# A hybrid decoder layer on one core: the first norm's factor from a token-layout copy of x, and another order of the first two projections

## The chip, the cores and the metric

One core of one Trainium2 chip runs the kernel. The metric is the device time of one execution in microseconds (us); lower is better. An instruction here runs on TensorE (PE: matrix products; PEld is its weight load), VectorE (DVE), ScalarE (ACT) or GpSimd (POOL); SyncE (SP) issues the DMA transfers. Each engine takes its instructions in the order in which the program gives them, and waits where an operand isn't there.

## The reference

`x` is 256 tokens of 1024 channels, in float32; the depth is one layer. The parts of the reference that matter here:

```python
def rms_norm(x, g):
    y = x * rsqrt(mean(x * x, axis=-1) + 1e-6)
    return y * g
...
h = rms_norm(x, pre_mix_g)                 # the first norm
u = h @ w_in                               # 1024 -> 2560 columns, split among four mixers
y_a = conformer_conv_mixer(u[:, :512])     # val * sigmoid(gate), causal conv of 31 taps, group norm, silu
...
y = concat([y_a, y_b, y_c, y_d]) @ w_out
x = x + rms_norm(y, post_mix_g)
m = square(relu(rms_norm(x, pre_mlp_g) @ mlp_w1)) @ mlp_w2
x = x + rms_norm(m, post_mlp_g)
```

The factor of the first norm, `rsqrt(mean(x*x) + eps)`, is one number for each token. It commutes with the projection, so the kernel multiplies it in after the product.

## The kernel before, in words

**Layout.** The first half of the kernel works in channel layout: 128 channels on the partitions, 256 tokens along a row. The weights come in chunks of 128 x 2048 float32 (1 MB) in the order of `seq` (line 87): ten chunks of `w_in`, four of `w_out`, then `w1` and `w2` in turn. Chunk number n is loaded by `load(n)` (SP), copied to a rounded half by `split_hi(n)` (ACT), and the rest is taken by `split_lo(n)` (DVE, `raw - hi`). A projection `proj(n)` (line 320) then makes three products for each of 8 channel blocks k and each of its two halves j: hi x hT, hi x hL, lo x hT, 48 products of 128x256 in all; `hT` and `hL` are the rounded half and the rest of `x * pre_mix_g`. So the third product of a half needs that half of the chunk's `lo`.

**Chunk 0** is different: its weights `w0` to `w7` come in the head (`hd`, lines 137 to 140, seven transfers) beside the blocks `x0` to `x7` of x in channel layout, and `native(k)` (line 189) makes its products in full float32, as four PE instructions for each k.

**The first norm's factor.** ACT squares the x blocks in pairs (`square`, line 208), DVE adds the results (`add`, line 211), and two products with a column of ones (`pss`, lines 254 to 256) sum over the partitions, which gives the sum of squares of each token on a partition. ACT takes the root with a scale and a bias, DVE the reciprocal (`rstd`), PE spreads it along a row with two transposes (`pr`, lines 261 to 263), and ACT copies that row to `R1` and its square to `R2`. In PE's order the `pss` products stand behind `native(4)`, the transposes behind `native(5)`.

**The first gate.** `conf_gate(t)` (line 364) multiplies a projection's gate half by `R1` on DVE into a tile `g` and takes its sigmoid on ACT. `conf_val(t)` (line 370) multiplies the value half by `R1` into the same tile `g`, which so has to wait for the sigmoid, then by the sigmoid into `zpad`, and ACT begins the convolution (`cacc`). The convolution's other taps (`run_taps`) fill DVE's time later.

**Order.** `InOrder` (line 50) keeps every engine's instructions in program order; the program is written out by hand at lines 555 to 659. Projections write to PSUM tiles of the tag `mm`, of which there are two, used in turn: `pu[3]`, the result of `proj(3)`, takes the place of `pu[1]` and so cannot be started before `conf_val(1)`, which stands behind `split_lo(3)` on DVE, has read `pu[1]`.

**Later.** `x` in token layout (`xs`, 2 x 512 KB) is loaded at lines 637 and 638 for the first residual. At the end (lines 957 to 964) PE makes twenty products of four shapes into a PSUM tile that nothing reads.

Of the kernel before, what the change touches and what calls it, by code (L numbers as in the profile page):

```python
# [16 lines left out]
F32 = mybir.dt.float32  # L17
F32R = mybir.dt.float32r
BF16 = mybir.dt.bfloat16
AF = mybir.ActivationFunctionType  # L20
ALU = mybir.AluOpType
# [3 lines left out]
P = 128  # L25
S = 256
D = 1024
KT = D // P
# [37 lines left out]
def hybrid_layer(ctx, tc, x, head, win, wout, w1, w2, gates, rows, out):  # L66
    nc = tc.nc
    V, A, G, T, Q = (InOrder(tc, e) for e in (nc.vector, nc.scalar, nc.gpsimd, nc.tensor, nc.sync))
# [4 lines left out]
    few = ctx.enter_context(tc.tile_pool(name="few", bufs=2))  # L73
    wk_ctx = tc.tile_pool(name="wk", bufs=1)
    wk = wk_ctx.__enter__()
# [4 lines left out]
    def sm(name):  # L80
        return psm.tile([P, 512], F32, tag="sm", name=name)

    def mm(name):
        return pmm.tile([P, 512], F32, tag="mm", name=name)


    seq = [("in", c) for c in (0, 1, 8, 5, 6, 7, 9, 3, 4, 2)]
# [6 lines left out]
    raw, hi, lo = {}, {}, {}  # L94

    def new_raw(n):
        k = seq[n]
        raw[k] = wts.tile([P, NW], F32, tag="raw", name=f"raw_{k[0]}{k[1]}")
        return raw[k], src[k[0]][k[1]]

    def load(n, parts=1):
        if n < len(seq):
            w, d = new_raw(n)
            for i in range(parts):
                c = slice(i * NW // parts, (i + 1) * NW // parts)
                Q.dma_start(w[:, c], d[:, c])

    def part(i, parts):
        return slice(i * NW // parts, (i + 1) * NW // parts)

    def split_hi(n, i=0, parts=1):
        if n < len(seq):
            k = seq[n]
            if i == 0:
                hi[k] = wts.tile([P, NW], F32R, tag="hi", name=f"hi_{k[0]}{k[1]}")
            c = part(i, parts)
            A.activation(hi[k][:, c], raw[k][:, c], AF.Copy)

    def split_lo(n, i=0, parts=1):
        if n < len(seq):  # L120
            k = seq[n]
            if i == 0:
                lo[k] = wts.tile([P, NW], F32R, tag="lo", name=f"lo_{k[0]}{k[1]}", bufs=3)
            c = part(i, parts)
            V.tensor_tensor(lo[k][:, c], raw[k][:, c], hi[k][:, c].bitcast(F32), op=ALU.subtract)
# [8 lines left out]
    xs = [cst.tile([P, D], F32, name=f"x{t}") for t in range(2)]  # L134
    gw = wk.tile([P, 4, P], F32, name="gw")
    c = 0
    for blocks in HEAD:
        n = HOFF[blocks[-1]] + S
        Q.dma_start(hd[:, c:n], head[:, c:n])
        c = n  # L140

    def hb(b):
        return hd[:, HOFF[b]:HOFF[b] + S]

    def xpair(k):
        a, b = HOFF[f"x{k}"], HOFF[f"x{k + 1}"] - HOFF[f"x{k}"]
        return hd[:, a:a + 2 * b].rearrange("p (k c) -> p k c", c=b)[:, :, :S]

    load(1, 2)
    load(2, 2)  # L150
    load(3)

# [2 lines left out]
    warm = cst.tile([P, 256], BF16, name="warm")  # L155
# [8 lines left out]
    eps_r = cst.tile([P, 1], F32, name="eps_r")  # L164
# [3 lines left out]
    ones = cst.tile([P, 1], F32, name="ones")  # L168
    G.memset(ones, 1.0)
    ident = cst.tile([P, P], F32, name="ident")  # L170
# [7 lines left out]
    hF = wts.tile([P, KT, S], F32, tag="hi", name="hF")  # L178
    hT = big.tile([P, KT, S], F32R, tag="hT", name="hT")
    hL = big.tile([P, KT, S], F32R, tag="hL", name="hL")  # L180
    sq = [wk.tile([P, 2, 2, S], F32, name="sq", tag=t) for t in ("sqx", "pTs")]
    sq = [q[:, i] for q in sq for i in range(2)]

    def bank(b, name):
        return mm(name) if b < 0 else pacc.tile([P, 512], F32, tag=f"acc{b}", name=name)

    pu0 = [bank(b, f"pu0_{j}") for j, b in enumerate((-1, 0))]

    def native(k):
        for j in range(2):  # L190
            T.matmul(pu0[j][:, :S], hb(f"w{k}")[:, j * P:(j + 1) * P], hF[:, k, :], start=(k == 0), stop=(k == KT - 1))
# [7 lines left out]
    e = wk.tile([P, 2], F32, name="e")  # L199
    sr = wk.tile([P, 2], F32, name="sr")  # L200
    s2 = wk.tile([P, 2], F32, name="s2")
    q = wk.tile([P, 2], F32, name="q_")
    A.preload_act_table(AF.Exp)

    def hf(k):
        V.tensor_scalar(hF[:, k, :], hb(f"x{k}"), hd[:, C_PRE + k:C_PRE + k + 1], None, op0=ALU.mult)

    def square(k):
        A.activation(sq[k // 2], xpair(k), AF.Square)

    def add(a, b):
        V.tensor_tensor(a, a, b, op=ALU.add)

    def h_hi(k):
        A.activation(hT[:, k:k + 2, :], hF[:, k:k + 2, :], AF.Copy)

    def h_lo(k):
        V.tensor_tensor(hL[:, k:k + 2, :], hF[:, k:k + 2, :], hT[:, k:k + 2, :].bitcast(F32), op=ALU.subtract)
# [1 line left out]
    hf(0)  # L220
    hf(1)
    V.tensor_scalar(nl, lam, -1.0, None, op0=ALU.mult)
    square(0)
    h_hi(0)
    hf(2)
    V.tensor_tensor(ab, nl, lam, op=ALU.max)
    A.activation(e, ab, AF.Exp, scale=-1.0)
    G.tensor_copy(prm, hd[:, :PCOLS])
    hf(3)
    square(2)  # L230
    hf(4)
    add(sq[0], sq[1])
    square(4)
    h_hi(2)
    hf(5)
    add(sq[0], sq[2])
    square(6)
    A.preload_act_table(AF.Sqrt)
    hf(6)
    hf(7)  # L240
    add(sq[0], sq[3])
    V.tensor_scalar(sr, e, 2.0, None, op0=ALU.add)
    add(sq[0][:, 0], sq[0][:, 1])
    V.reciprocal(sr, sr)
    h_hi(4)
    h_hi(6)
    h_lo(0)
    h_lo(2)
    for k in range(5):
        native(k)  # L250
    R1 = cst.tile([P, S], F32, name="R1")
    R2 = cst.tile([P, S], F32, name="R2")
    rstd = cst.tile([P, 2], F32, name="rstd")
    pss = sm("pss")
    for t in range(2):
        T.matmul(pss[:, t:t + 1], sq[0][:, 0, t * P:(t + 1) * P], ones, start=True, stop=True)
    A.activation(rstd, pss[:, 0:2], AF.Sqrt, bias=eps_r, scale=1.0 / D)
    V.reciprocal(rstd, rstd)
    h_lo(4)
    native(5)  # L260
    pr = sm("pR")
    for t in range(2):
        T.transpose(pr[:, t * P:(t + 1) * P], rstd[:, t:t + 1].to_broadcast([P, P]), ident)
    native(6)
    native(7)

    zpad = wk.tile([P, 2, CK - 1 + S], F32, name="zpad")
    G.memset(zpad[:, :, :CK - 1], 0.0)
# [4 lines left out]
    identb = cst.tile([P, P], BF16, name="identb")  # L273
# [43 lines left out]
    def two(pu):  # L317
        return pu.rearrange("p (j t) -> p j t", j=2)

    def proj(n, between=None):  # L320
        c = seq[n][1]
        pu = mm(f"pu{c}")
        H, L = hi["in", c], lo["in", c]
        for j in range(2):
            if j and between:
                between()
            o = pu[:, j * S:(j + 1) * S]
            for k in range(KT):
                ws = slice(j * 1024 + k * P, j * 1024 + (k + 1) * P)
                T.matmul(o, H[:, ws], hT[:, k, :], start=(k == 0), stop=False)  # L330
                T.matmul(o, H[:, ws], hL[:, k, :], start=False, stop=False)
                T.matmul(o, L[:, ws], hT[:, k, :], start=False, stop=(k == KT - 1))
        return two(pu)

    def proj_v(n):
# [28 lines left out]
    def conf_gate(t):  # L364
        g = st["cg", t] = wk.tile([P, S], F32, name="cg", tag="la")
        V.tensor_tensor(g, pu[t][0], R1, op=ALU.mult)
        s = st["sig", t] = wk.tile([P, S], F32, name="sig", tag="lt")
        A.activation(s, g, AF.Sigmoid)

    def conf_val(t):  # L370
        g = st["cg", t]
        V.tensor_tensor(g, pu[t][1], R1, op=ALU.mult)
        V.tensor_tensor(zpad[:, t, CK - 1:], g, st["sig", t], op=ALU.mult)
# [42 lines left out]
    def scaled(o, pu, r=None):  # L416
        V.tensor_tensor(o, pu, (R1 if r is None else r)[:, None, :].to_broadcast([P, 2, S]), op=ALU.mult)

# [136 lines left out]
    pu = {}  # L555

    load(4)
    split_hi(1, 0, 2)
    A.activation(R1, pr[:, :S], AF.Copy)
    split_lo(1, 0, 2)  # L560
    h_lo(6)
    split_hi(1, 1, 2)
    A.preload_act_table(AF.Sigmoid)
    A.activation(R2, R1, AF.Square)
    pu[0] = [p_[:, :S] for p_ in pu0]
    conf_gate(0)
    split_lo(1, 1, 2)

    pu[1] = proj(1)
    pu[1] = [pu[1][:, t] for t in range(2)]  # L570
    split_hi(2, 0, 2)
    conf_val(0)
    split_hi(2, 1, 2)
    split_lo(2, 0, 2)
    run_taps(2, 0)
    split_lo(2, 1, 2)
    split_hi(3)

    pu[2] = proj(2)
# [54 lines left out]
    att_ptrans()  # L634
    run_taps(2)
    lru_scan()
    Q.dma_start(xs[0], x[0:P, :])
    Q.dma_start(xs[1], x[P:, :])

    pu[8] = proj(8)  # L640
    split_lo(9)
# [195 lines left out]
    wk = ctx.enter_context(tc.tile_pool(name="wk2", bufs=2))  # L837
# [41 lines left out]
    cols = {(t, h): half(h) for t in range(2) for h in range(2)}  # L879
# [7 lines left out]
    for n in range(14, len(seq)):  # L887
        name, c = seq[n]
# [10 lines left out]
        if n == 14:  # L899

            for t in range(2):
                scr = few.tile([P, D], BF16, name="scr", bufs=1)
# [52 lines left out]


    pb = mm("shapes")
    H15 = hi["w2", 15]
    wide_zeros = warm[:, None, :].to_broadcast([P, 2, 256])
    for lhs, rhs, n in ((H15[:, :P], H15[:, 512:1024], 512), (identb, wide_zeros, 512), (H15[:, :P], H15[:, 512:896], 384),  # L960
                        (H15[:, :P], H15[:, 512:576], 64)):
        for _ in range(5):
            T.matmul(pb[:, :n] if rhs is not wide_zeros else pb.rearrange("p (a b) -> p a b", a=2), lhs, rhs,
                     start=True, stop=True)


# [41 lines left out]
```

## Time and profile before

| what | value |
|---|---|
| median of 3 runs | 288.17 us (287.48 to 288.68) |
| profiled execution, its own time | 288.29 us |
| span of that execution, first to last instruction | 286.6 us |
| PE busy | 279.3 us, 97% |
| DVE busy | 193.6 us, 68% |
| ACT busy | 152.6 us, 53% |
| POOL busy | 22.3 us, 8% |
| DMA | 53.04 MB, mean 185 GB/s |

A timeline row gives the start, the duration, the engine, the line, the operation and its tiles (out <- in), the shapes, and after x how many instructions the row merges; brackets hold idle time of the engine just before and what ended it. All instructions carry line 60, since one helper issues them, so the tiles tell them apart. A matmul's end is modelled; its start is what counts. A DMA row gives the number of issues, KB of each and the median time from issue to landing.

### The profile page before, as it was taken

The numbers are of one execution on the slowest core, as the hardware profiler recorded it, in microseconds if no ns is written. First come the engines' busy times: TensorE is split into PE (matmuls) and PEld (weight loads), VectorE is DVE, ScalarE is ACT, GpSimd is POOL, SyncE is SP. The second block draws the span as 40 slices with busy tenths as digits, with TensorE's granted clock in tenths as the row PEclk, the third lists the DMA queues.
The fourth block names the chain that finished last, engine by engine and source line by source line (L and its number), as shares of the span: only waits on it lengthen the run. The fifth ranks groups of instructions, "written<-read, shape, count | busy, mean of one in ns | idle before, by whom it ended". The sixth has DMA issues, their size and how long they took to land.

```text
span 286.6 us, 4726 instructions
## 1 busy us (share of the span) xinstructions
PE 279.3 (97%) x1954; PEld 255.9 (89%) x1954; DVE 193.6 (68%) x262; ACT 152.6 (53%) x192; POOL 22.3 (8%) x53
## 2 busy tenths in 40 slices
PE   6799999999999999999999999999999999999995
PEld 4699997999977899989999899899899899899883
DVE  1999999899989996765636646546447357257262
ACT  3995459875548849642632623624615515526141
POOL 4388500000000000000000000000000000000000
PEclk9999999999999999999999999999999999999999
DMA  6999446926404544675374383472472562600012
GB/s 210 412 409 334 150 156 225 411 74 238 146 2 153 213 150 173 266 287 214 101 281 166 129 293 133 165 293 96 199 287 74 226 255 69 266 0 0 2 73 74
DMA packets 9237, 53.04 MB, mean 185 GB/s; under 512 B 1024, under 2 KB 1536, under 8 KB 3712
## 3 DMA queue, kind: packets, MB, share of 16 engines
q1 hardware_dynamic: 9216, 52.75, 49.1%
q8 instruction: 15, 0.25, 0.3%
q14 instruction: 6, 0.05, 0.1%
HBM read 51.70 MB, written 1.05 MB: 184 GB/s over the span
## 4 chain that ended last, share of the span: by engine, by line
PE 94%; DMA 2%; DVE 1%; SPq 0%; ACT 0%; issue 0%
PE acd L60 31%; PE pm L60 29%; PE pu L60 19%; PE acc L60 7%; DMA hd<-in_head_dram 2%; PE pz L60 2%; PE shapes L60 1%; PE psc L60 1%; PE po L60 1%; DVE sq L60 1%; PE pg L60 1%; PE pth L60 0%; PE ptp L60 0%; SPq L60 0%; PE pvar L60 0%; DVE hF L60 0%
## 5 line engine op out<-in xcount | busy, mean ns | idle before, releaser
L60 DVE TENSOR_TENSOR lo_w<-raw_w,hi_w 128x2048 fp32r<-128x2048 f32 (+2 forms) x36 | 72.6, 2050 | 17.8 <-ACT hi_w L60 17.8
L60 PE MATMUL pm<-h2L,hi_w 128*128 128x256 f32 x240 | 66.5, 277 | 0.0
L60 PE MATMUL pm<-h2T,hi_w 128*128 128x256 f32 x240 | 66.5, 277 | 0.0
L60 PE MATMUL pm<-h2T,lo_w 128*128 128x256 f32 x240 | 66.4, 277 | 0.0
L60 ACT ACTIVATE hi_w<-raw_w 128x2048 fp32r<-128x2048 f32 (+1 forms) x33 | 59.6, 1849 | 1.3 <-issue 1.3
L60 PE MATMUL acd<-hi_w,ml 128*128 128x512 f32 (+1 forms) x160 | 56.0, 350 | 0.0
L60 PE MATMUL acd<-lo_w,mh 128*128 128x512 f32 (+1 forms) x160 | 55.8, 349 | 0.0
L60 PE MATMUL acd<-hi_w,mh 128*128 128x512 f32 (+1 forms) x160 | 55.8, 348 | 0.0
L60 ACT ACTIVATE mr<-pm 128x512 f32<-128x512 f32 x15 | 8.9, 596 | 73.8 <-PE pm L60 73.8
L60 PEld LDWEIGHTS pm<-h2T,hi_w 128*128 128x128 f32 x240 | 45.1, 188 | 0.0
L60 PEld LDWEIGHTS pm<-h2T,lo_w 128*128 128x128 f32 x240 | 45.1, 188 | 0.0
L60 PEld LDWEIGHTS pm<-h2L,hi_w 128*128 128x128 f32 x240 | 45.1, 188 | 0.0
L60 DVE TENSOR_TENSOR mr<-mr 128x512 f32<-128x512 f32 x16 | 11.1, 693 | 44.7 <-ACT mr L60 44.7
L60 PE MATMUL pu<-hT,hi_in 128*128 128x256 f32 x128 | 36.3, 284 | 0.0
L60 PE MATMUL pu<-hT,lo_in 128*128 128x256 f32 x128 | 35.9, 280 | 0.0
L60 PE MATMUL pu<-hL,hi_in 128*128 128x256 f32 x128 | 35.9, 280 | 0.0
L60 PEld LDWEIGHTS acd<-lo_w,mh 128*128 128x128 f32 x160 | 30.2, 189 | 4.2
L60 PEld LDWEIGHTS acd<-hi_w,ml 128*128 128x128 f32 x160 | 30.1, 188 | 4.2
L60 PEld LDWEIGHTS acd<-hi_w,mh 128*128 128x128 f32 x160 | 30.1, 188 | 4.1
L60 DVE SCALAR_TENSOR_TENSOR cacc<-zpad,prm,cacc 128x256 f32<-128x256 f32 x60 | 25.3, 477 | 0.1
L60 PEld LDWEIGHTS pu<-hT,hi_in 128*128 128x128 f32 x128 | 24.3, 190 | 0.0
L60 PEld LDWEIGHTS pu<-hT,lo_in 128*128 128x128 f32 x128 | 24.2, 189 | 0.0
(177 smaller groups left out, 381.3 us busy)
## 6 DMA issues: line engine op xcount, KB each, us to landing
raw_w<-in_w_dram SPq DMA_DIRECT2D x32, 1024.0 KB, 4.9
raw_in<-in_win_dram SPq DMA_DIRECT2D x7, 1024.0 KB, 5.6
raw_out<-in_wout_dram SPq DMA_DIRECT2D x4, 1024.0 KB, 4.9
raw_in<-in_win_dram SPq DMA_DIRECT2D x4, 512.0 KB, 7.9
hd<-in_head_dram SPq DMA_DIRECT2D x3, 384.0 KB, 5.9
x<-in_x_dram SPq DMA_DIRECT2D x2, 512.0 KB, 7.5
grow<-in_rows_dram SPq DMA_DIRECT2D x2, 512.0 KB, 7.1
hd<-in_head_dram SPq DMA_DIRECT2D x2, 256.0 KB, 4.9
```

The costliest lines, as they stand in the source:

```text
L60: ins = f(*args, **kwargs)
```

## The change

It loads x in token layout early, between chunk 1 and chunk 2, and no longer at lines 637 and 638. The squares, adds and ones-products go; ACT squares each of the two token tiles with a running sum instead (`token_rstd`). The products of chunk 0 stand in one go on PE. Chunk 1's products (`proj_passes`) go pass by pass, all hi x hT of a half, then all hi x hL, then all lo x hT, with the transposes behind the first pass of the second half. The `hi` of chunk 1 is made as two quarters and a half, and chunk 2's first half is split ahead of `conf_gate(0)`, its second half behind it. Chunk 0's two PSUM tiles are `acc0` and `acc1` instead of one `mm` and `acc0`. The unread products at the end are six of 256 columns, one of 2, six of 256 and six of 512.

```diff
     load(1, 2)
+    for t in range(2):
+        Q.dma_start(xs[t], x[t * P:(t + 1) * P, :])
     load(2, 2)
     load(3)
...
-    sq = [wk.tile([P, 2, 2, S], F32, name="sq", tag=t) for t in ("sqx", "pTs")]
-    sq = [q[:, i] for q in sq for i in range(2)]
...
-    pu0 = [bank(b, f"pu0_{j}") for j, b in enumerate((-1, 0))]
+    pu0 = [bank(b, f"pu0_{j}") for j, b in enumerate((0, 1))]
...
     hf(3)
-    square(2)
-    hf(4)
-    add(sq[0], sq[1])
-    square(4)
+    A.preload_act_table(AF.Sqrt)
     h_hi(2)
-    hf(5)
-    add(sq[0], sq[2])
-    square(6)
-    A.preload_act_table(AF.Sqrt)
-    hf(6)
-    hf(7)
-    add(sq[0], sq[3])
-    V.tensor_scalar(sr, e, 2.0, None, op0=ALU.add)
-    add(sq[0][:, 0], sq[0][:, 1])
-    V.reciprocal(sr, sr)
+    for k in range(4, KT):
+        hf(k)
     h_hi(4)
     h_hi(6)
-    h_lo(0)
-    h_lo(2)
-    for k in range(5):
+    V.tensor_scalar(sr, e, 2.0, None, op0=ALU.add)
+    V.reciprocal(sr, sr)
+    for k in range(KT):
         native(k)
+    for k in range(0, KT, 2):
+        h_lo(k)
...
-    pss = sm("pss")
-    for t in range(2):
-        T.matmul(pss[:, t:t + 1], sq[0][:, 0, t * P:(t + 1) * P], ones, start=True, stop=True)
-    A.activation(rstd, pss[:, 0:2], AF.Sqrt, bias=eps_r, scale=1.0 / D)
-    V.reciprocal(rstd, rstd)
-    h_lo(4)
-    native(5)
-    pr = sm("pR")
-    for t in range(2):
-        T.transpose(pr[:, t * P:(t + 1) * P], rstd[:, t:t + 1].to_broadcast([P, P]), ident)
-    native(6)
-    native(7)
+    def token_rstd():
+        ss0 = few.tile([P, 2], F32, name="ss0", bufs=1)
+        for t in range(2):
+            scr = few.tile([P, D], BF16, name="scr", bufs=1)
+            A.activation(scr, xs[t], AF.Square, accum_out=ss0[:, t:t + 1])
+        A.activation(rstd, ss0, AF.Sqrt, bias=eps_r, scale=1.0 / D)
+        V.reciprocal(rstd, rstd)
+    def row_of_rstd():
+        pr = sm("pR")
+        for t in range(2):
+            T.transpose(pr[:, t * P:(t + 1) * P], rstd[:, t:t + 1].to_broadcast([P, P]), ident)
+        A.activation(R1, pr[:, :S], AF.Copy)
+        A.activation(R2, R1, AF.Square)
...
+    def proj_passes(n, between):
+        c = seq[n][1]
+        pu = mm(f"pu{c}")
+        H, L = hi["in", c], lo["in", c]
+        for j in range(2):
+            o = pu[:, j * S:(j + 1) * S]
+            for i, (w, h) in enumerate(((H, hT), (H, hL), (L, hT))):
+                for k in range(KT):
+                    ws = slice(j * 1024 + k * P, j * 1024 + (k + 1) * P)
+                    T.matmul(o, w[:, ws], h[:, k, :], start=(i == 0 and k == 0), stop=(i == 2 and k == KT - 1))
+                if j and i == 0:
+                    between()
+        return two(pu)
...
     load(4)
-    split_hi(1, 0, 2)
-    A.activation(R1, pr[:, :S], AF.Copy)
+    split_hi(1, 0, 4)
+    split_hi(1, 1, 4)
+    split_hi(1, 1, 2)
     split_lo(1, 0, 2)
-    h_lo(6)
-    split_hi(1, 1, 2)
+    split_lo(1, 1, 2)
+    token_rstd()
     A.preload_act_table(AF.Sigmoid)
-    A.activation(R2, R1, AF.Square)
+    split_hi(2, 0, 2)
+    split_lo(2, 0, 2)
+    pu[1] = proj_passes(1, row_of_rstd)
+    pu[1] = [pu[1][:, t] for t in range(2)]
     pu[0] = [p_[:, :S] for p_ in pu0]
     conf_gate(0)
-    split_lo(1, 1, 2)
-    pu[1] = proj(1)
-    pu[1] = [pu[1][:, t] for t in range(2)]
-    split_hi(2, 0, 2)
+    split_hi(2, 1, 2)
     conf_val(0)
-    split_hi(2, 1, 2)
-    split_lo(2, 0, 2)
+    split_lo(2, 1, 2)
     run_taps(2, 0)
-    split_lo(2, 1, 2)
     split_hi(3)
     pu[2] = proj(2)
...
-    Q.dma_start(xs[0], x[0:P, :])
-    Q.dma_start(xs[1], x[P:, :])
...
-    H15 = hi["w2", 15]
-    wide_zeros = warm[:, None, :].to_broadcast([P, 2, 256])
-    for lhs, rhs, n in ((H15[:, :P], H15[:, 512:1024], 512), (identb, wide_zeros, 512), (H15[:, :P], H15[:, 512:896], 384),
-                        (H15[:, :P], H15[:, 512:576], 64)):
-        for _ in range(5):
-            T.matmul(pb[:, :n] if rhs is not wide_zeros else pb.rearrange("p (a b) -> p a b", a=2), lhs, rhs,
-                     start=True, stop=True)
+    H15, L15 = hi["w2", 15], lo["w2", 15]
+    def unread(n, cols):
+        for i in range(n):
+            T.matmul(pb[:, :cols], (H15, L15)[i % 2][:, i * P:(i + 1) * P], H15[:, 1024:1024 + cols], start=True, stop=True)
+    unread(6, 256)
+    T.matmul(pb[:1, :2], warm[:, :1], warm[:, :2], start=True, stop=True)
+    unread(6, 256)
+    unread(6, 512)
```

Behind this stretch the program is as before: `proj(2)`, `conf_gate(1)`, one tap, `split_lo(3)`, `split_hi(4)`, `conf_val(1)`, `proj(3)` and so on.

## Rows read from the trace of the kernel before

**Rows 1.** Page, part 4: the chain that ended last, by engine.

```profile
PE 94%; DMA 2%; DVE 1%; SPq 0%; ACT 0%; issue 0%
```

**Rows 2.** Timeline of PE, 7 to 15 us.

```profile
7.52 2.86 PE L60 MATMUL pu<-hF,hd 128*128 128x256 f32 x12 [0.97 <-DVE hF L60]
...
11.64 0.58 PE L60 MATMUL pss<-ones,sq 128*128 128x1 f32 x4 [1.27 <-DVE sr L60]
...
13.03 0.38 PE L60 MATMUL pR<-ident,rstd 128*128 128x128 f32 x2
...
14.79 0.47 PE L60 MATMUL pu<-hT,hi_in 128*128 128x256 f32 x1
```

**Rows 3.** Timeline of PE: the first products of proj(2) and of proj(3).

```profile
20.63 0.28 PE L60 MATMUL pu<-hT,hi_in 128*128 128x256 f32 x1
...
26.28 0.28 PE L60 MATMUL pu<-hT,hi_in 128*128 128x256 f32 x1
```

**Rows 4.** SP's issues, landing times by window of issue, DMA rate in one us.

```profile
4.21 1.49 SPq L60 DMA_DIRECT2D raw_in<-in_win_dram  x2
...
raw_in<-in_win_dram SPq DMA_DIRECT2D x2, 512.0 KB, 7.4
...
7.10 1.31 SPq L60 DMA_DIRECT2D raw_in<-in_win_dram  x2
...
raw_in<-in_win_dram SPq DMA_DIRECT2D x1, 512.0 KB, 8.1
...
10.00:11.00 1.00, 0.38 (x2) 0.00 (x0) 1.00 (x4) 1.00 (x1) 0.00 (x0) 1.00 1.03 414
```

**Rows 5.** Timeline of ACT, 9 to 24 us.

```profile
9.87 1.28 ACT L60 ACT_TABLE_LOAD   x1
11.16 1.15 ACT L60 ACTIVATE hT<-hF 128x512 fp32r<-128x512 f32 x2
12.32 0.26 ACT L60 ACTIVATE rstd<-pss,eps_r 128x2 f32<-128x2 f32 x1
...
16.41 0.40 ACT L60 ACTIVATE sig<-cg 128x256 f32<-128x256 f32 x1
16.72 1.04 ACT L60 ACTIVATE hi_in<-raw_in 128x1024 fp32r<-128x1024 f32 x1
...
18.36 2.85 ACT L60 ACTIVATE hi_in<-raw_in 128x1024 fp32r<-128x1024 f32 x2
...
21.83 1.90 ACT L60 ACTIVATE hi_in<-raw_in 128x2048 fp32r<-128x2048 f32 x1
```

**Rows 6.** Timeline of ACT, 109 to 113 us: a square with a running sum.

```profile
110.09 1.05 ACT L60 ACTIVATE scr<-x 128x1024 bf16<-128x1024 f32 x1
111.03 0.19 ACT L60 ACTIVATION_READ_ACCUMULATOR scr<-x 128x1 f32 x1
```

**Rows 7.** Timeline of DVE, 17 to 25 us.

```profile
17.80 1.23 DVE L60 TENSOR_TENSOR lo_in<-raw_in,hi_in 128x1024 fp32r<-128x1024 f32 x1
...
19.86 1.22 DVE L60 TENSOR_TENSOR lo_in<-raw_in,hi_in 128x1024 fp32r<-128x1024 f32 x1
20.99 0.42 DVE L60 TENSOR_TENSOR cg<-pu,R 128x256 f32<-128x256 f32 x1
...
21.72 2.29 DVE L60 TENSOR_TENSOR lo_in<-raw_in,hi_in 128x2048 fp32r<-128x2048 f32 x1
23.92 0.42 DVE L60 TENSOR_TENSOR cg<-pu,R 128x256 f32<-128x256 f32 x1
```

**Rows 8.** Timeline of the end, DVE and PE, and landing of the last store.

```profile
280.89 1.54 DVE L60 SCALAR_TENSOR_TENSOR u<-u,r,x 128x384 f32<-128x384 f32 x3
...
281.50 1.71 PE L60 MATMUL shapes<-hi_w 128*128 128x384 f32 x10
...
out_dram<-u SPq DMA_DIRECT2D x1, 128.0 KB, 2.9
```

**Rows 9.** Timeline of PE, the start: the warm-up products.

```profile
1.16 2.74 PE L60 MATMUL warm<-warm 128*128 128x256 bf16 x12 [1.16 <-POOL eps_r L60]
```

More of the change, by code (lines that the diff above doesn't have):

```diff
@@ L206, in hf @@
         V.tensor_scalar(hF[:, k, :], hb(f"x{k}"), hd[:, C_PRE + k:C_PRE + k + 1], None, op0=ALU.mult)
[L208 to L212, printed above, removed]
     def h_hi(k):
@@ L222, in hybrid_layer @@
     V.tensor_scalar(nl, lam, -1.0, None, op0=ALU.mult)
-    square(0)
     h_hi(0)
```

## The prediction

> **What bounds the kernel now.** I read the chain of waits first: 94% of the span is PE, and the rest lies at the start and the end [rows 1]. So the change can only pay where PE waits. PE's timeline at the start comes next: the last product of `native(4)` ends at 10.38, by the model of the ends, and `pss` starts at 11.64, after 1.27 us of waiting for DVE's adds [rows 2]. From there PE hardly stops: chunk 1 begins at 14.79 [rows 2], `proj(2)` at 20.63, `proj(3)` at 26.28 [rows 3]. Between these two lie 48 products in 5.65 us, 0.118 us each. Then I read what DVE, ACT and the DMA do in these 26 us, because after the change PE asks earlier for what they make. The question is how late `proj(3)` starts: behind it the program is the same, and PE stays the bound.
>
> **Removed.** Four squares, four adds and `pss`: PE loses the wait of 1.27 and the 0.58 of `pss` [rows 2]. `native(2)` to `native(4)` are 12 instructions in 2.86 us, so `native(2)` to `native(7)` are 24 in 5.7 at most, and chunk 1 may start by 7.52 + 5.7 = 13.2 instead of 14.79. The 32 products up to the transposes take 3.8, to 17.0. The row's two transposes (0.38 [rows 2]) and 16 more products bring PE to 19.3, where `proj(2)` started at 20.63: a lead of 1.3 us. Now what it meets.
>
> **Transfers.** Before, the second part of chunk 2 was issued at 7.10 and landed 8.1 later, at 15.2 [rows 4]. In SP's order x's two tiles, 512 KB each, stand exactly where chunk 2's two parts stood, so I put the second tile at 15.2 and the first one piece earlier: 0.52 MB at the 414 GB/s of this stretch [rows 4] is 1.27, so 13.9. Everything behind lands 1 MB, 2.5 us, later. Chunk 2's parts then come at 16.5 and 17.7, ahead of their use below. Chunk 3 was there by about 19.4, since ACT took it without a pause [rows 5], so 21.9 at the latest; it is wanted at 22.5. The raw halves of chunk 1 were issued at 4.21 and about 5.0 and took 7.4 [rows 4], so 11.6 and 12.4, and ACT's two quarters and a half (some 2.1 by the 1.04 of a half [rows 5]) are done by 14.5, before the second x tile is there. The old load of x at lines 637 and 638 goes; no wait for a DMA stands on the chain there, so that gives 0.
>
> **The factor's new chain.** ACT squares the second x tile at 15.2: 1.13 with the read of the sum, from 110.09 to 111.03 and 0.19 more [rows 6], so 16.35. The root takes 0.26 [rows 5], to 16.65; DVE's reciprocal lets PE's transposes go at 16.9, so PE, there at 17.0, hardly waits. But behind the root on ACT stand the sigmoid's table load, 1.28, and chunk 2's first `hi`, 1.04 [rows 5]: 17.95 and 19.0. DVE then takes the first `lo`, 1.23 [rows 7]: 20.25. `proj(2)` needs it for its third product, so that starts at 20.3, against 20.63 + 0.24 = 20.87 before. PE has waited about 0.8 and 0.6 of its lead is left.
>
> The table load costs 1.28 and nothing more in the row: the next instruction starts at 11.16, where the load ends at 9.87 + 1.28 [rows 5]. The Trainium skill (ScalarE: Activation LUTs, What ACT_TABLE_LOAD costs) says that a switch also has a drain of some 1380 ns; with it my chain would end near 290.8 instead of 289.4. The trace speaks against that.
>
> **The queue behind it.** `conf_gate(0)`, whose sigmoid ran at 16.41 before [rows 5], now follows the first `lo` on DVE. Its product may start at 20.16 (1.13 after the `lo`, as from 19.86 to 20.99 [rows 7]) and takes 0.42, to 20.58. ACT's sigmoid (0.40 [rows 5]) is over at 21.0. Only then may `conf_val(0)` write the same tile (0.42, to 21.5) and `zpad` (by its size 0.42 more, to 21.95). ACT, which holds chunk 2's second `hi` behind the sigmoid, has it at 21.0 + 1.04 = 22.05. So the second `lo` runs from 22.05 to 23.27. PE reaches its use at 20.3 + 24 x 0.118 = 23.1, waits 0.15, and ends `proj(2)` at 25.9.
>
> From the start of the second `lo` on I take DVE's own pace: 1.13 to the next start, 0.93 for two taps (from 17.80 to 19.86 less the 1.13), 0.73 for the gate's product of chunk 1 and a tap (20.99 to 21.72), 2.20 for `split_lo(3)` (21.72 to 23.92) [rows 7]. Together 4.99. ACT keeps up: `cacc`, and chunk 3's `hi` (1.9 [rows 5]) from 22.6 to 24.5, before DVE's `lo` at 24.85. So `conf_val(1)` starts at 27.04, where it started at 23.92 [rows 7], and has read `pu[1]` at 27.46. **`proj(3)` waits for that**, because its PSUM tile is that of `pu[1]`: it starts at 27.5, against 26.28. Before, this wait was hidden by 26.28 - 24.34 = 1.9 us. What is late next is `split_lo(4)`, at 31.9; PE wants it at 33.2. DVE then trails PE by 1 us more than before and has several us in hand.
>
> **Free edits.** The other PSUM tiles of chunk 0 are free at the start. More issues on SP before chunk 2: two issues take 1.5 us of SP's time [rows 4], under landing times of 7 us; 0. The unread products: the last store follows DVE's last piece, 280.89 + 1.54 = 282.4, and takes 2.9 to land, to 285.3, while the old products end at 281.50 + 1.71 = 283.2 [rows 8]. The new ones are fewer columns and start no later; 0. Were that cover gone, 1 us of them would show.
>
> **The sum.** 27.5 - 26.28 = **+1.2 us**: 1.3 of lead at `proj(2)` given up for waits of 0.8, 0.15 and 1.6. The profiled execution would read 288.29 + 1.2 = 289.5; it stands 0.12 above the median, so I forecast **289.4**. Bounds, for what the trace doesn't show in this place: x's second tile a piece sooner, 1.27 less (it can't pass chunk 1, so no better), gives 288.1; an extra 1.28 on ACT, as long as one more table load, gives 290.7. I take the middle, since the slot, the sizes and the rate are those of the rows.
>
> **Rivals.** *PE's lead survives (0.16).* If x lands a piece sooner and `conf_gate(0)` meets no wait for the sigmoid (0.6 of my 8 us from the first `lo` to 27.04 is waiting), DVE reaches `conf_val(1)` at 25.2. PE then ends `proj(2)` near 25.4 without a wait, and `proj(3)` starts 0.5 or so sooner than before: 287.7, not slower. It decides where the second x tile lands before 14.0. The saturated rate and the order of issue [rows 4] speak against it; the landing times are of transfers with other neighbours, so it isn't excluded.
>
> *The table switch costs double (0.07).* The sigmoid's load stands right behind the root on the new chain; anything that holds ACT there passes straight to `proj(3)`. One more 1.28 makes 290.7. Against it: the rows above show no pause. The skill's drain would be this case.
>
> *The clock falls (0.08).* After the change PE waits about 0.8, 0.15 and 1.6 us within ten. Before, it stood 1.27 idle before `pss` [rows 2], and the clock granted from 10 to 11 us is 1.00 [rows 4] (the third number from the end of that row). But the warm-up products, 256 columns as well, came every 2.74/12 = 0.23 us [rows 9], twice the 0.118 of `proj`: the lower of the two levels, 1.2 GHz, after an idle start. A spell of that length loses half of 2.74, 1.4 us: 290.8. The Trainium skill (TensorE: Matmul & The Clock Gate, HAM oscillation) has idle gaps between bursts as the cause of such falls; no row here shows one in mid-kernel.
>
> **How the numbers follow.** The forecast has 0.62, the three rivals 0.31, and 0.07 is left for what I don't see. The range must hold 8 in 10: 287.7 (the first rival) to 290.9 (the bound of the chain and the clock's case). A measurement of this kernel can tell about 0.5%, 1.44 us, from no change. My forecast, +0.42%, lies inside that, but close to its edge: with some 0.7 us of doubt either way, four in ten of its chance is slower by over 0.5% (0.25), the rest (0.37) within. The second and third rivals add 0.15 to slower; the first is mostly within (0.10), and 0.06 beyond on the fast side; the remainder is spread 0.05 on faster, 0.02 on slower. That makes faster 0.11, within 0.47, slower 0.42.
>
> **What would show it.** In the changed profile: the squares of `scr` near 13.9 and 15.2; a table load from 16.65; PE's first chunk-1 product near 13; the third product of `proj(2)` at 20.3, released by DVE's `lo`; the second `lo` starting at 22; above all PE idle for about 1.6 before `proj(3)`, released by DVE's `cg`, and `proj(3)` at 27.5. The prediction is wrong if `proj(3)` starts at 26.3 or sooner, if x lands by 14, or if a stretch behind 28 us takes back what the start lost.

## The result

| kernel | median | runs | lowest to highest |
|---|---|---|---|
| before, run beside the change | 287.59 us | 12 | 286.46 to 288.68 |
| changed | 289.44 us | 12 | 289.04 to 289.90 |

The ratio is 1.0063, with a 95% interval of 1.0049 to 1.0077: the change makes the kernel slower, by 1.85 us. The profiled execution of the changed kernel took 289.11, its span is 287.0, and the granted clock is 1.00 throughout. The interval includes the 0.5% that was taken as the limit of what can be told, and lies above no change as a whole.

The page of the changed kernel, the span, the busy times and the chain that ended last:

```profile
span 287.0 us, 4704 instructions
PE 279.0 (97%) x1949; PEld 254.7 (89%) x1949; DVE 191.2 (67%) x258; ACT 153.5 (53%) x193; POOL 16.6 (6%) x53
PE 89%; DVE 3%; DMA 2%; POOL 2%; ACT 2%; issue 1%; SPq 1%; POOLq 0%
```

PE's share of the chain fell from 94% [rows 1] to 89%; DVE and ACT came in; POOL's 2% is the first wait below, which DVE ends. PE's busy time barely moved, so the loss is waiting. PE's timeline at the four places where it waits or starts a stage, to be held against [rows 2, 3]:

```profile
12.13 0.47 PE L60 MATMUL pu<-hT,hi_in 128*128 128x256 f32 x1
...
17.12 0.41 PE L60 MATMUL pR<-ident,rstd 128*128 128x128 f32 x2 [1.00 <-POOL q__137 L60]
...
20.46 0.38 PE L60 MATMUL pu<-hT,lo_in 128*128 128x256 f32 x1 [0.76 <-DVE lo_in L60]
...
27.82 0.39 PE L60 MATMUL pu<-hT,hi_in 128*128 128x256 f32 x1 [1.46 <-DVE cg L60]
```

Chunk 1 starts at 12.13 instead of 14.79, so PE leads by 2.7 us. About 0.85 of that is the head, not the change: PE's long row of chunk 0's products begins at 6.67 here and at 7.52 in [rows 2], since the blocks of x landed sooner in this execution. PE then waits 1.00 for the transposes, 0.76 for the third product of `proj(2)` and 1.46 for `proj(3)`, which starts at 27.82 instead of 26.28. The first of these rows names POOL as the releaser, but the transposes read `rstd` from DVE. DVE's reciprocal, in the second fence below, ends at 16.98, 0.14 before them.

ACT's and DVE's timelines of the same stretch show what PE waited for:

```profile
13.89 1.06 ACT L60 ACTIVATE scr<-x 128x1024 bf16<-128x1024 f32 x1 [0.23 <-DMA x<-in_x_dram]
14.86 0.19 ACT L60 ACTIVATION_READ_ACCUMULATOR scr<-x 128x1 f32 x1
15.24 1.06 ACT L60 ACTIVATE scr<-x 128x1024 bf16<-128x1024 f32 x1 [0.20 <-DMA x<-in_x_dram]
16.20 0.19 ACT L60 ACTIVATION_READ_ACCUMULATOR scr<-x 128x1 f32 x1
16.48 0.29 ACT L60 ACTIVATE rstd<-ss,eps_r 128x2 f32<-128x2 f32 x1
16.80 1.28 ACT L60 ACT_TABLE_LOAD   x1
18.09 1.06 ACT L60 ACTIVATE hi_in<-raw_in 128x1024 fp32r<-128x1024 f32 x1
...
20.78 0.42 ACT L60 ACTIVATE sig<-cg 128x256 f32<-128x256 f32 x1 [0.91 <-DVE cg L60]
21.10 1.04 ACT L60 ACTIVATE hi_in<-raw_in 128x1024 fp32r<-128x1024 f32 x1
```

```profile
16.81 0.17 DVE L60 RECIPROCAL rstd<-rstd 128x2 f32<-128x2 f32 x1 [1.89 <-ACT rstd L60]
19.18 1.23 DVE L60 TENSOR_TENSOR lo_in<-raw_in,hi_in 128x1024 fp32r<-128x1024 f32 x1 [2.21 <-ACT hi_in L60]
20.33 0.42 DVE L60 TENSOR_TENSOR cg<-pu,R 128x256 f32<-128x256 f32 x1
21.23 0.43 DVE L60 TENSOR_TENSOR cg<-pu,R 128x256 f32<-128x256 f32 x1 [0.48 <-ACT sig L60]
...
22.18 1.27 DVE L60 TENSOR_TENSOR lo_in<-raw_in,hi_in 128x1024 fp32r<-128x1024 f32 x1
23.37 1.13 DVE L60 SCALAR_TENSOR_TENSOR cacc<-zpad,prm,cacc 128x256 f32<-128x256 f32 x2
24.42 0.42 DVE L60 TENSOR_TENSOR cg<-pu,R 128x256 f32<-128x256 f32 x1
...
25.15 2.28 DVE L60 TENSOR_TENSOR lo_in<-raw_in,hi_in 128x2048 fp32r<-128x2048 f32 x1
27.35 0.41 DVE L60 TENSOR_TENSOR cg<-pu,R 128x256 f32<-128x256 f32 x1
```

It is one chain to read from top to bottom: x lands, square, root, table load, `hi`, `lo`, gate, sigmoid, second `hi`, second `lo`, taps, gate of chunk 1, `split_lo(3)`, `conf_val(1)`. DVE stands idle for 1.89 and 2.21 us in it, waiting for ACT, and then has no time left to catch up before PE wants `proj(3)`.

### The profile page after: what moved, and what is told of

Its sections match the earlier page's. It is cut to its first block, busy times and chain, and to the rows that moved or that the text cites. A ratio compares the mean times of both kernels' runs of the same rounds, so it can differ in the third digit from the quotient of the medians.

```text
span 287.0 us, 4704 instructions
## 1 busy us (share of the span) xinstructions
PE 279.0 (97%) x1949; PEld 254.7 (89%) x1949; DVE 191.2 (67%) x258; ACT 153.5 (53%) x193; POOL 16.6 (6%) x53
## 3 DMA queue, kind: packets, MB, share of 16 engines
HBM read 51.70 MB, written 1.05 MB: 184 GB/s over the span
## 4 chain that ended last, share of the span: by engine, by line
PE 89%; DVE 3%; DMA 2%; POOL 2%; ACT 2%; issue 1%; SPq 1%; POOLq 0%
PE acd L60 31%; PE pm L60 29%; PE pu L60 13%; PE acc L60 7%; DMA hd<-in_head_dram 2%; PE pz L60 2%; POOL q__137 L60 2%; DVE lo_in L60 1%; PE psc L60 1%; PE shapes L60 1%; PE po L60 1%; ACT hi_in L60 1%; PE pg L60 1%; SPq L60 1%; DVE cacc L60 1%
## 5 line engine op out<-in xcount | busy, mean ns | idle before, releaser
L60 PE MATMUL pu<-hT,hi_in 128*128 128x256 f32 x128 | 33.7, 281 | 1.5 <-DVE cg L60 1.5
L60 PE MATMUL pu<-hT,lo_in 128*128 128x256 f32 x128 | 33.4, 279 | 0.8 <-DVE lo_in L60 0.8
L60 PE MATMUL pu<-hL,hi_in 128*128 128x256 f32 x128 | 33.2, 278 | 0.0
L60 PEld LDWEIGHTS pu<-hT,hi_in 128*128 128x128 f32 x128 | 23.1, 188 | 1.7 <-DVE cg L60 1.7
L60 PEld LDWEIGHTS pu<-hT,lo_in 128*128 128x128 f32 x128 | 23.1, 188 | 1.2 <-DVE lo_in L60 1.2
```

Of the source, the lines that this page charges most:

```text
L60: ins = f(*args, **kwargs)
```

## The experiments

The theory: the end of the run is set by the start of `proj(3)`, and that start by the chain from x's landing through ACT and DVE. The rivals: the other unread products cost something; the early transfers delay chunks 2 and 3; the PSUM bank alone makes the wait; and, found in the traces on the way, the place of the operands in SBUF.

### The old unread products in the changed kernel, and the new ones in the kernel before

```diff
-    unread(6, 256)
...
+    for lhs, rhs, n in ((H15[:, :P], H15[:, 512:1024], 512), (identb, wide_zeros, 512), ...
```

> The changed kernel with the twenty old unread products at the end in place of the nineteen new ones. Theory (the wait before proj(3) is the whole loss): the same as the changed kernel, 289.4 within 0.4, proj(3) at 27.8. Rival (the other unread products cost what the chain does not explain: the medians lie 1.85 apart, the starts of proj(3) 1.54): about 0.3 to 0.4 less, 289.0 to 289.1, and the time outside the span back from 2.1 to 1.7.

> The kernel before with the nineteen new unread products alone. Theory: no change against the kernel before, within 0.4, proj(3) at 26.28. Rival (unread products): 0.3 to 0.4 slower, with 2.1 instead of 1.7 between the execution's time and its span.

Measured: the changed kernel with the old ones 289.03, ratio to the kernel before 1.0051 (1.0035 to 1.0067); the kernel before with the new ones 287.72, ratio 0.9999 (0.9975 to 1.0023). `proj(3)` starts at 27.81 in the first and 25.74 in the second, where I had 26.28 for it; what moves that start stands further down. The time outside the span, a profiled execution's own time less its span, follows the rest of the kernel, 2.1 in the first and 1.7 in the second, against the rival. The median of the first, 289.03, is what the rival gave, but its ratio and the change's own overlap widely, and the second shows no cost. So no trace puts a part of the loss on the unread products; a few tenths of a us can't be told either way.

### The early load of x alone

```diff
     load(1, 2)
+    for t in range(2):
+        Q.dma_start(xs[t], x[t * P:(t + 1) * P, :])
     load(2, 2)
...
-    Q.dma_start(xs[0], x[0:P, :])
-    Q.dma_start(xs[1], x[P:, :])
```

> The kernel before with x's two token tiles loaded between chunks 1 and 2, nothing else. Theory: chunk 2 lands at 16.5 and 17.7, chunk 3 at 20.2 instead of 17.7, so DVE's split of chunk 3 starts some 0.4 to 0.9 later, inside the 1.9 of room before proj(3): proj(3) at 26.3, no change within 0.4. Rival (the transfers alone make the delay): proj(2) or proj(3) starts 1 or more later, 288.6 or more.

Measured: 287.02 against 287.62, ratio 0.9978 (0.9956 to 1.0001). ACT did wait for chunk 3, but the wait fell into the room before `proj(3)`, which starts at 26.01:

```profile
20.14 1.92 ACT L60 ACTIVATE hi_in<-raw_in 128x2048 fp32r<-128x2048 f32 x1 [1.01 <-DMA raw_in<-in_win_dram]
```

The transfers show no cost by themselves. The median is even 0.6 lower; in the profile the end of the run is about 1.0 shorter (last section).

### The kernel before, with its own sum, but PE's new order

```diff
-    for k in range(5):
+    for k in range(KT):
         native(k)
...
-    native(5)
-    pr = sm("pR")
...
+    split_hi(1, 0, 4)
+    h_lo(4)
+    root()
+    split_hi(1, 1, 4)
+    h_lo(6)
+    split_lo(1, 0, 2)
+    split_hi(1, 1, 2)
+    def gate0():
+        A.preload_act_table(AF.Sigmoid)
+        A.activation(R2, R1, AF.Square)
+        conf_gate(0)
+        split_lo(1, 1, 2)
+    pu[1] = proj_passes(1, {0: row_of_rstd, 2: gate0})
```

`root` is the square root and the reciprocal; `row_of_rstd` makes the transposes and `R1`; both callbacks stand in the first half of chunk 1, behind its first and its third pass. As in the changed kernel, chunk 0's products go to `acc0` and `acc1`. The squares and adds stay as they were.

> The kernel before with its own squares, adds and ones-products, but all products of chunk 0 in one go, the ones-products behind them, and chunk 1 pass by pass with the transposes behind the first pass of its first half. Theory (PE's lead was sound, the factor's new chain gave it away): the factor is there by 13.5, PE starts chunk 1 near 13, proj(2) near 19.2 and proj(3) near 24.8, because conf_val(1) has read its tile by 24.5; 1.3 to 1.5 faster than the kernel before, about 286.2. Rival (DVE's own work sets proj(3) in any order): proj(3) stays near 26.3 and the time is that of the kernel before.

Measured: 285.71 us, ratio 0.9939 (0.9915 to 0.9962): 1.9 faster than the kernel before and 3.7 below the changed kernel. The factor is there at 13.4; DVE reads `pu[1]` from 24.27 on, and `proj(3)` starts at 24.75 without a wait that the trace would show. DVE's rows, with the start of the first `lo` of chunk 2 at 18.14 instead of 19.18 and `conf_val(1)` three us sooner than in the changed kernel:

```profile
13.22 0.17 DVE L60 RECIPROCAL rstd<-rstd 128x2 f32<-128x2 f32 x1 [0.33 <-ACT rstd L60]
...
18.14 1.22 DVE L60 TENSOR_TENSOR lo_in<-raw_in,hi_in 128x1024 fp32r<-128x1024 f32 x1
...
22.06 2.29 DVE L60 TENSOR_TENSOR lo_in<-raw_in,hi_in 128x2048 fp32r<-128x2048 f32 x1
24.27 0.42 DVE L60 TENSOR_TENSOR cg<-pu,R 128x256 f32<-128x256 f32 x1
```

So PE's lead was sound, and it was given away on the factor's new way through x's landing and ACT, which is longer than the squares and adds that it replaces: the reciprocal starts at 13.22 here and at 16.81 in the changed kernel. Only part of the 1.9 is the lead, though. `proj(3)` starts at 25.28 to 26.28 in the five profiles whose start is that of the kernel before, so at 24.75 it is 0.5 to 1.5 sooner; about 1.0 more lies at the end of the run, 6.0 from the last needed product to the end for 6.8 and 7.0 in the two profiles of the kernel before, where the program is the same (last section). That is why 1.9 came out where 1.3 to 1.5 was expected. The two orders also differ in more than the sum: here the transposes stand in chunk 1's first half and the gate of chunk 0 ahead of chunk 2's first `lo`, and no run separates this from the factor.

### The sigmoid's table load behind chunk 2's first hi

```diff
     token_rstd()
-    A.preload_act_table(AF.Sigmoid)
     split_hi(2, 0, 2)
+    A.preload_act_table(AF.Sigmoid)
```

> The changed kernel with the sigmoid's table load behind chunk 2's first hi instead of ahead of it. Theory (the chain root, table load, hi, lo sets proj(2), and what queues behind it proj(3)): the first lo starts 1.25 sooner, at 17.9, proj(2) no longer waits for it, the second lo starts 0.7 to 0.8 sooner, since the gate's sigmoid still waits for the load, and proj(3) starts at 27.0 to 27.1: 0.7 to 0.8 less than the changed kernel, 288.7. Rival (DVE's total work sets proj(3), wherever the load stands): 27.8 and 289.4.

Measured: 288.41, ratio to the kernel before 1.0015 (0.9998 to 1.0033), about 1.0 below the changed kernel. In the profile:

```profile
15.49 1.06 ACT L60 ACTIVATE scr<-x 128x1024 bf16<-128x1024 f32 x1 [0.20 <-DMA x<-in_x_dram]
...
16.94 1.04 ACT L60 ACTIVATE hi_in<-raw_in 128x1024 fp32r<-128x1024 f32 x1
18.00 1.28 ACT L60 ACT_TABLE_LOAD   x1
```

```profile
27.25 0.39 PE L60 MATMUL pu<-hT,hi_in 128*128 128x256 f32 x1 [1.53 <-DVE cg L60]
```

x landed 0.25 later here than in the changed kernel's profile; less that, `proj(3)` starts at 27.0, 0.8 sooner, as expected. The first `lo` starts at 18.01 and `proj(2)` no longer waits for it, but the wait before `proj(3)` is as long as before: PE is 0.6 sooner too. One edit of order wins back a little over half of the loss by the medians, which come from separate sets of runs, and three quarters by the ratios (1.0015 for 1.0063), so the load's place on the chain is shown.

### The result of proj(3) in another PSUM bank

```diff
-    pu[3] = proj(3)
+    pu[3] = proj(3, b=2)
```

`proj` takes the number of the bank as an argument here; nothing else changes.

> The changed kernel with the result of proj(3) in the PSUM bank of acc2, which is free, so that it need not wait until conf_val(1) has read pu[1]. Theory (DVE is late as a whole): two products start at 25.9, the third waits for split_lo(3) until 27.45, so only 0.3 to 0.6 are won, 288.9 to 289.1. Rival (the bank alone is the wait): proj(3) goes on at 25.9 and 1.6 or more are won, 287.8 or less.

Measured: 288.64, ratio 1.0030 (1.0014 to 1.0045), 0.8 below the changed kernel by the medians and 0.38 by the profiled executions. PE:

```profile
26.44 0.28 PE L60 MATMUL pu<-hT,hi_in 128*128 128x256 f32 x1
26.55 0.28 PE L60 MATMUL pu<-hL,hi_in 128*128 128x256 f32 x1
27.80 0.39 PE L60 MATMUL pu<-hT,lo_in 128*128 128x256 f32 x1 [0.98 <-DVE lo_in L60]
```

Two products go ahead, and the third waits for `split_lo(3)`. x's second square starts 0.32 later here (15.56 for 15.24); with that the profiles differ by 0.7, near the 0.8 of the medians and a little over the 0.3 to 0.6 expected. So the bank was the last of two late things: `split_lo(3)` ends at 27.75 here, and `conf_val(1)` has read `pu[1]` at 28.09, 0.34 later. The free bank wins those 0.34 and about two products' time. The rest of the loss stays, because DVE's queue as a whole is late.

### Where ss0 lies

From 114 to 281 us thirty products of a `w2` chunk take 5.64 us in the changed kernel and 5.59 in the kernel before, sixteen times over. The program of that stretch is the same. One such link in the chain of waits of the kernel before (start, length, engine, output, line, products):

```profile
124.76 5.59 PE acd L60 x30
```

The link that answers to it in the chain of the changed kernel:

```profile
125.57 5.64 PE acd L60 x30
```

The changed kernel has one small tile more in the pool `few`, `ss0`; the program opens the pool `wk` behind `few`. Two edits move that tile alone, apart from one clear of it by POOL at the start in the second:

```diff
-        ss0 = few.tile([P, 2], F32, name="ss0", bufs=1)
+        ss0 = wk.tile([P, 2], F32, name="ss0")
```

```diff
+    pad = few.tile([P, 2], F32, name="ss0", bufs=1)
+    G.memset(pad, 0.0)
     eps_r = cst.tile([P, 1], F32, name="eps_r")
```

> The changed kernel with its one new small tile, ss0 (8 bytes a partition), in the pool wk instead of the pool few, so that the tiles of the pools behind few lie where they lay before. Found in the traces: from 114 to 281 us thirty products of a w2 chunk take 5.64 in the changed kernel and with the old unread products, 5.59 in the four traces without ss0: 0.9 over sixteen chunks. Theory (the place of the operands in SBUF): 5.59 again, 288.5. Rival (the later start or the order of the first products sets the pace): 5.64, 289.4.

> The kernel before with an unused tile of 8 bytes a partition more in the pool few, cleared once by POOL, as ss0 shifts the pools behind it. Theory (the place of the operands in SBUF): thirty products of a w2 chunk take 5.64 instead of 5.59, 0.9 slower than the kernel before, 288.5. Rival (nothing but order and start matter): 5.59 and the time of the kernel before.

> The changed kernel with ss0 in the pool wk once more, for a profile of an undisturbed execution. Theory (the place of the operands in SBUF sets the pace of the w2 products): thirty products of a w2 chunk take 5.59, not 5.64. Rival (order and start set it): 5.64.

Measured: `ss0` in `wk` 289.07 over ten executions, ratio 1.0046 (1.0026 to 1.0065). An eleventh, the profiled one, took 980 us; the rows are from a second profile, 289.41. The kernel before with the unused tile: 287.78, ratio 1.0007 (0.9988 to 1.0026). The same link in the chain of the kernel before with the tile:

```profile
123.15 5.64 PE acd L60 x30
```

And in the chain of the changed kernel with `ss0` in `wk`:

```profile
126.49 5.59 PE acd L60 x30
```

The pace follows the tile both ways, so where the tile lies sets it: that much is shown. That it acts through the place of these products' own operands is not. By the program, `mh` and `ml`, which the `w2` products multiply, lie in pools opened behind `few`, and the weights in one opened ahead of it; no trace shows an address.

But the time does not follow. Ahead of the `w2` stretch the same tile has the opposite effect on 96 products, those of `proj(6)` and `proj(7)`. Their link in the chain of the kernel before and in that of the changed kernel:

```profile
48.33 11.31 PE pu L60 x96
```

```profile
49.56 10.90 PE pu L60 x96
```

It is 10.90 in all six traces with the tile in `few` and 11.31 in all seven without, though the weights and `hT`, `hL` of these products lie in pools opened ahead of `few`. So the tile costs 0.9 in the `w2` stretch and gives back 0.4 here. With `ss0` in `wk` two more projections got slower, 5.65 for 5.46 and 5.71 for 5.52, another 0.4. From the start of `proj(3)` to the first `w2` product it is 25.28 to 111.86 = 86.6 in the kernel before with the tile, 87.1 without it at the same pace of the first projections (25.48 to 112.58, next section), and 28.07 to 115.42 = 87.4 in the changed kernel with `ss0` in `wk`, against 27.82 to 114.29 = 86.5 with it in `few`. My expectation of 0.9 in the total was wrong for the kernel before with the tile, whose interval excludes it; for `ss0` in `wk` the interval takes in both theory and rival, and the traces say nearly nothing is won.

### Both kernels profiled again

> The kernel before, profiled a second time. Theory (its start hangs on when the head's blocks land, which differs between executions; the pace belongs to the program): the third block of x is scaled between 5.7 and 6.7 instead of 7.11, proj(3) starts between 25.7 and 26.1, its products come 0.118 apart, thirty w2 products take 5.59. Rival (the start is fixed): 7.1 and 26.3 again. If the pace is drawn anew in each execution, it may be 0.113.

> The changed kernel, profiled a second time. Theory (x's landing heads the chain, and it varies little): proj(3) between 27.7 and 28.1 with 1.3 to 1.7 of PE idle before it, thirty w2 products in 5.64. If the pace behind the wait is a property of the program, 0.113 again; if it is drawn anew in each execution, it may be 0.118, as with the old unread products.

| profile | proj(3) starts | products of proj(3), proj(4) apart | proj(3) to the end of the last needed product | that end to the end of the span | outside the span | time |
|---|---|---|---|---|---|---|
| before | 26.28 | 0.118 | 253.3 | 7.0 | 1.7 | 288.29 |
| before again | 25.48 | 0.113 | 253.0 | 6.8 | 1.7 | 287.02 |
| changed | 27.82 | 0.113 | 253.3 | 5.9 | 2.1 | 289.11 |
| changed again | 28.48 | 0.113 | 253.1 | 6.0 | 2.0 | 289.64 |

The columns are worked out from the timelines and chains of the four profiles; the last needed product is the one ahead of the unread ones. The middle column is nearly constant, 252.9 to 253.7 in twelve traces, all but that of the other bank, where `proj(3)` starts and then waits. So `proj(3)`'s start is a fair measure of the whole. But it is constant because unequal parts cancel, as the section before and the last paragraph of the next one show. In the second profile of the changed kernel x landed later, its second square starting at 15.89 instead of 15.24, and `proj(3)` moved by 0.66, to 28.48, beyond the 27.7 to 28.1 expected. In the second profile of the kernel before, the third block of x was scaled at 6.44 instead of 7.11, chunk 1 started at 14.39 instead of 14.79, and `proj(3)` 0.8 sooner, at 25.48 where I had 25.7 at the soonest. Half of this 0.8 is the landing; the other half is the pace, which I expected to be the program's: the 96 products from chunk 1 to `proj(3)` take 11.09 for 11.49. So both kernels hang on landings, the kernel before on the pace as well, and the profile shown before the prediction was the latest of five.

### A second version of the faster order

```diff
-    h_lo(4)
-    root()
     split_hi(1, 1, 4)
+    h_lo(4)
+    root()
...
-        g = st["cg", t]
+        g = wk.tile([P, S], F32, name="cv", tag="rg")
```

> The kernel before with chunk 0 in one go and the ones-products behind it, as tried, and two waits less: the root behind the second quarter of chunk 1's hi on ACT, so that PE's first pass isn't cut in two (0.7 lost there), and a tile of its own for the product of conf_val, so that DVE doesn't wait for the sigmoid (0.48). Theory (DVE's queue and PE's lead together set proj(3)): proj(3) starts at 24.2 to 24.4 instead of 24.75, 285.3. Rival (ACT's second hi of chunk 2 sets it): proj(3) at 24.7 and 285.7 again.

Measured: 285.60, ratio 0.9931 (0.9914 to 0.9948), the same as the first version within the intervals. DVE's `split_lo(3)` starts at 21.58, 0.5 sooner, as meant; yet `proj(3)` starts at 24.84. From 19.19 on PE makes the 48 products of `proj(2)` 0.118 apart without a gap, so neither DVE nor ACT sets `proj(3)` any more, but PE's own pace in that execution. Neither theory had that.

## Why the prediction came out right, and which terms were off

The forecast of 289.4 met 289.44, and slower by over 0.5% had 0.42. The steps, one by one, against the first profile of the changed kernel:

- **PE's lead.** Right, and larger than the bound: chunk 1 at 12.13, where I had 13.2 at the latest. Of the 1.07, 0.85 is the head's earlier landing in this execution. The lead was of no use: I had PE hardly waiting for the transposes, and it waited 1.00, because they came at 17.12, near my 17.0, however early PE was there.
- **x's landing.** I put the squares at 13.9 and 15.2; they started at 13.89 and 15.24. The transfers took over the slots of chunk 2's parts, and the transfers alone show no cost.
- **The chain.** Root at 16.48, table load at 16.80, first `lo` at 19.18, third product of `proj(2)` at 20.46, for 16.4, 16.65, 19.0 and 20.3. ACT goes on within 0.03 before the load and 0.01 after it. So the drain of some 1380 ns that the Trainium skill (ScalarE: Activation LUTs, What ACT_TABLE_LOAD costs) states is not seen in this place, and the second rival falls.
- **The queue behind it.** Second `lo` at 22.18 for 22.05, `conf_val(1)` at 27.35 for 27.04. Most of the missing 0.2 is the two taps, 1.05 to the next start where I had 0.93. `proj(3)` at 27.82 for 27.5: the step was undersized by 0.3, the sum of many hand-overs of a few hundredths and the taps.
- **The bank.** That `proj(3)` waits for `pu[1]` is what the row names. The other bank showed that this hides a second late thing at once, `split_lo(3)`, which ends at 24.85 + 2.29 = 27.14 by my own figures and which I should have named as the price of that reading.
- **The rivals.** PE's lead did not survive: the second x tile did not land before 14.0, its square started at 15.24. The clock did not fall: the granted clock stayed at 1.00 through the waits, and the products behind them came 0.113 to 0.118 apart. The second sign is the better one, since the granted clock also reads 1.00 from 1 to 4 us, where the warm-up products of [rows 9] came 0.23 apart.
- **The free edits.** The unread products: no cost was seen either way, as forecast. But "behind it the program is the same" was too simple: it set four terms behind `proj(3)` at nothing, and none of them is. The last paragraph of this section has them. My own sign of being wrong, a stretch behind 28 us that takes back what the start lost, came true by half.

**The size of the difference** was off: +1.2 was forecast and +1.85 measured. That the time still met the forecast to 0.04 is luck: the base lay 0.6 lower, the difference 0.65 higher. The three runs shown had a median of 288.17, twelve have 287.59, and the profile that I started from took 288.29. I took `proj(3)` at 26.28 as the kernel's own; five profiles with that start have 25.28 to 26.28. Chunk 1 starts between 14.19 and 14.79 in them, as the head lands, and the 96 products up to `proj(3)` take 11.09 or 11.49. Against the two profiles each, the start moved by 28.15 - 25.88 = 2.3, the end gave back about 1.0, and the outside took 0.35: 1.65, near the 1.85. The term that was off is the base: one execution's landing times and pace were taken as fixed. The doubt of 0.7 covered it.

In the profile pair alone the account closes: +1.54 at `proj(3)`, -0.97 up to the first `w2` product (113.72 to 114.29 is only +0.57), +0.90 in the `w2` stretch, -1.07 at the end, +0.42 outside: +0.82, which is 289.11 - 288.29. Of the 0.97, 0.41 is `proj(6)` and `proj(7)`, 0.31 the pace of `proj(3)` and `proj(4)`, and 0.24 four transposes near 103 us, 0.60 for 0.83. The four terms behind `proj(3)` take back 0.72 together.

## What to carry to other kernels

Before a sum is moved to another engine to spare the bound one a wait, follow what stands behind the new sum on that engine: here the table load and the next chunk's split stood behind the root, and DVE's whole queue behind those. Moving the consumers instead, the products of chunk 0 ahead of the ones-products, gave the lead without the new chain, and about 1 of the 1.9 us that this order measured; the other 1 came from the end of the run. When one profile is the base of a forecast, look where its own time stands among the runs, and which of its early starts hang on a landing or on the pace of that execution.

## What the runs showed of the hardware that was not expected

- The same stretch of products runs at one of two paces: 0.113 or 0.118 us from one product of 256 columns to the next, all through `proj(3)` and `proj(4)`. The two profiles of the kernel before have one each, 0.118 and 0.113, so it is not a property of the program; the second version of the faster order has 0.118 and the first 0.113. Over 192 products, four projections, it is 0.9 us, as much as half of the loss studied here. In the first 40 us of these traces the pace changes only behind a pause of PE: `proj(2)` of the changed kernel runs at 0.114 in its first half and at 0.118 from 23.50 on, behind a pause of 0.2 us, and `proj(3)` at 0.113 behind the wait of 1.46. The kernel before makes some 190 products from 15 us on without a pause and holds one pace through all of them. What decides which of the two it is stays open.
- A tile of 8 bytes a partition in an earlier pool changed the pace of products 100 us later by 0.9%, 5.59 to 5.64, in both directions of the test, and sped up 96 others from 11.31 to 10.90. Those two are 0.118 and 0.1135 for a product, the same two paces, so there the tile decides between them. Which tile's place matters was not tried.
- The last store, 128 KB, took 2.9 us to land in the kernel before and 1.9 in the changed one. The issues of the store at the end of the kernel before:

```profile
out_dram<-u SPq DMA_DIRECT2D x2, 192.0 KB, 2.0
out_dram<-u SPq DMA_DIRECT2D x1, 128.0 KB, 2.9
```

  And in the changed kernel:

```profile
out_dram<-u SPq DMA_DIRECT2D x2, 192.0 KB, 1.9
out_dram<-u SPq DMA_DIRECT2D x1, 128.0 KB, 1.9
```

  It was 2.7 in the second profile of the kernel before, 3.0 with the unused tile, and 1.9 with x loaded early and in both versions of the faster order. That is the 1 us at the end of the run. The unread products are not its cause, since the kernel before with the new ones has 2.9. One thing goes with it: the queue q14, of the kind that the page calls instruction, has six packets within the span of the four profiles with 2.7 to 3.0, and five in the ten others. The rows of the kernel before and of the changed kernel:

```profile
q14 instruction: 6, 0.05, 0.1%
```

```profile
q14 instruction: 5, 0.04, 0.0%
```

  The sixth packet, 8 KB, starts at 283.75 in the kernel before, while the last store is under way; none falls there in the ten others. That it holds the store up is likely but not shown: no run moves it alone.
- The time outside the span is 2.0 to 2.1 in every profile of the changed kernel and its variants, and 1.7 to 1.85 in all others, the early x, the unused tile and PE's new order among them. Of the parts of the change that leaves the token-layout sum with its tile, and the order of the splits; no run separates further.
